# One projection's last 128 columns with exchanged operands, and a bias in a copy, in a two-layer decoder on one core

## The chip, the cores and the metric

One NeuronCore of a Trainium2 chip runs the whole program in one launch. The time is device time in microseconds. Below it is abbreviated us. The kernel before takes 1340.01 us (median of three runs, 1339.97 to 1340.18). The engines are named as in the profile: PE is the matrix engine, PEld its weight loads, DVE the vector engine, ACT the scalar engine, POOL GpSimd, and SP the engine that issues most DMAs; a "q" behind a name (SPq, ACTq) means the instruction stream that issues DMAs there.

## The reference

The input x has 2048 positions of 1024 features, in 32-bit floats. Layer 0 normalises x (RMSNorm), makes four projections of it, B, C, h and G, forms `(B * conv3(C * h)) * silu(G)` with a causal convolution of width 3, and adds its projection to x. From this stream, x1, a shared K and V come out of one projection. Layer 1 makes a query and a gate, runs stick-breaking attention with 8 heads of 64, and ends so:

```python
z = jnp.einsum("bhqd,bhkd->bhqk", qb, kf[:, :, :kl]) * scale
log_one_minus = jnp.where(mask, jax.nn.log_sigmoid(-z), 0.0)
rev = lax.cumsum(log_one_minus, axis=3, reverse=True)
weights = jnp.exp(jnp.where(mask, z + rev, -jnp.inf))
o = jnp.einsum("bhqk,bhkd->bhqd", weights, vf[:, :, :kl])
x = x + (o * jax.nn.silu(g)) @ w_out_b[j]
return _rmsnorm(x, norm_f)
```

The sum over the attention weights telescopes, so the kernel computes the output as "first v" (the value at a fixed position beside each block of queries) plus a product of the remaining weights with differences of neighbouring values.

## The kernel before

**Layout.** Everything lies transposed: features on the 128 partitions, positions along the free axis, in reversed order. The 2048 positions are four chunks (`c` = 0 to 3) of 512 columns (`CH`); 1024 features are eight blocks of 128 (`KD`, index `ob` or `k`). A full-precision product is built from split operands: each operand is kept as a high part and the rest (`split`, tiles of type float32r), and three matmuls (high with high, high with rest, rest with high) are added in PSUM; `mm3` does that over the contraction blocks. One matmul multiplies a stationary 128x128 block by a moving 128x512 block.

**Stages.** Layer 0's projections (tiles `fa_C`, `fa_B` and the like) use a scheme of seven products in place of eight, then comes its output projection (`fa_o`), the pair K/Q and V/G (`fa_kq`, `fa_vg`), then attention per chunk and head (`attend`, line 1056) and the last projection (`pob`): `out_kept` with `norm_kept` for chunks 0 to 2, and `out_last` (line 1328) for chunk 3.

**One head of attention.** PE makes `z`, ACT takes the sigmoid into `R`, POOL masks it, DVE scans it, PE transposes it into `wt`, ACT and DVE split it into `wth` and `wtl`, and PE multiplies by V into `av`. There is one PSUM bank for `av` (`NAV` is 1, line 32). `av` leaves it in two steps: an ACT copy of one half of its partitions into `ot`, then a DVE addition of the other half. The next head's first `av` matmul needs both done. After two heads `gate_kept` (line 1276) lets POOL add `v_first` to `ot` by blocks of 128 columns and multiply by the gate `sga`; for chunks 2 and 3 `split_og` then makes the operands `og` on ACT and DVE.

**The last chunk.** For each block `ob`, `out_last` runs 12 matmuls into `pob`, DVE adds them to `x`, ACT squares `x` into `sq_x` and scales `x` by the last norm's gain. The squares of the first five blocks are summed by POOL into `acc_x`; that sum and the last three squares go through matmuls with a column of ones into `pst_x`, four columns of it, one for each 128 positions. `rsqrt` turns these into reciprocal roots by 12 small DVE instructions in a row, each needing the one ahead (`v_x`, `t_x`, `yr_x`), `bcast` spreads them over the partitions by four transposes (`prb_x`, and once more as `prb_x23s` for ACT's copy `pbs`), and DVE (six blocks) and POOL (two) multiply `x`. Eight DMAs of 256 KB, half from SP and half from ACT's queue, write the output. Behind them comes a branch on a flag (line 1421) to a fallback that isn't taken with these inputs.

**Order.** The kernel is not issued in the order in which it is written. All operations are recorded (so nearly all have line 363 in the profile: tiles tell them apart), each belongs to a named part (`a30` is chunk 3's head 0, `g30` its first gate, `o3` is `out_last`, `fold` the splitting of the last weights), and `PLAN` gives each part two keys, between which its operations get their priorities. A list planner (`order`, line 290) goes through time with a price for each operation (`cost`, line 214), always taking the operation that can start first and, among those, the one with the lowest key. The result is one fixed instruction order for each engine, and every engine executes its own strictly in that order, waiting where an operand is late.

## Time and profile before

| what | before |
|---|---|
| median of three runs | 1340.01 us |
| the profiled execution, its own time | 1341.83 us |
| its span, first to last instruction | 1340.0 us |
| mean granted PE clock | 0.993 of full |
| PE busy | 1302.8 us, 97% |
| DVE busy | 1016.9 us, 76% |
| ACT busy | 599.7 us, 45% |
| POOL busy | 435.5 us, 33% |

The span runs from the first to the last instruction. Rows of groups give the line, engine, operation, output<-input, shapes and count, then busy time and the mean duration of one in ns, then the idle time of that engine just ahead and what ended it. The chain of waits follows the work back from the last instruction. A row of the stretches view begins with the stretch, its length, then busy us and count for PE, PEld, DVE, ACT and POOL, the PE clock granted, the DMA share and GB/s. In the order of time a row gives start, length, engine, and what ran.

### The profile page before, as it was taken

The numbers are of one execution on the slowest core, as the hardware profiler recorded it, in microseconds if no ns is written. First come the engines' busy times: TensorE is split into PE (matmuls) and PEld (weight loads), VectorE is DVE, ScalarE is ACT, GpSimd is POOL, SyncE is SP. The second block draws the span as 40 slices with busy tenths as digits, with TensorE's granted clock in tenths as the row PEclk, the third lists the DMA queues.
The fourth block names the chain that finished last, engine by engine and source line by source line (L and its number), as shares of the span: only waits on it lengthen the run. The fifth ranks groups of instructions, "written<-read, shape, count | busy, mean of one in ns | idle before, by whom it ended". The sixth has DMA issues, their size and how long they took to land.

```text
span 1340.0 us, 18973 instructions
## 1 busy us (share of the span) xinstructions
PE 1302.8 (97%) x6184; PEld 1078.0 (80%) x6184; DVE 1016.9 (76%) x1607; ACT 599.7 (45%) x1052; POOL 435.5 (33%) x553
## 2 busy tenths in 40 slices
PE   8999999999999999999999989999999999999996
PEld 6888888888888888888787777788778887788885
DVE  7899866689964655656869578877998886797855
ACT  7344534444432332323334334554555553566643
POOL 5252000001000000010032355334357675547982
PEclk9999999999999999999999999999999999999997
DMA  9439879878898799987998976887687567999734
GB/s 326 170 130 326 283 271 325 282 278 295 306 355 289 253 356 330 325 289 244 352 322 314 310 260 209 266 264 236 223 301 255 185 209 227 335 367 300 264 106 159
DMA packets 215292, 364.99 MB, mean 272 GB/s; under 512 B 16996, under 2 KB 101008, under 8 KB 215184
## 3 DMA queue, kind: packets, MB, share of 16 engines
q1 hardware_dynamic: 214464, 362.61, 79.4%
q8 instruction: 51, 0.84, 0.2%
q10 hardware_dynamic: 592, 1.05, 0.2%
q14 instruction: 57, 0.47, 0.1%
q0 software_dynamic: 128, 0.02, 0.0%
HBM read 217.35 MB, written 146.28 MB: 271 GB/s over the span
## 4 chain that ended last, share of the span: by engine, by line
PE 78%; DVE 12%; issue 4%; DMA 2%; POOL 2%; ACT 1%; SPq 0%; DVEq 0%; POOLq 0%; ACTq 0%
PE fa_C L363 11%; PE fa_B L363 10%; PE fa_o L363 6%; PE fd_C L363 6%; PE pob L363 5%; PE fd_B L363 5%; PE fa_kq L363 5%; PE fa_vg L363 4%; PE fe_C L363 3%; PE fd_vg L363 3%; PE fe_B L363 3%; PE fd_o L363 3%; PE fd_kq L363 3%; PE av L363 2%; PE wt L363 1%
## 5 line engine op out<-in xcount | busy, mean ns | idle before, releaser
L363 POOL COPY halo<-p 128x2 f32<-128x2 f32 x32 | 15.1, 472 | 435.2 <-DVE p L363 435.2
L363 POOL TENSOR_TENSOR acc_x<-acc_x,sq_x 128x512 f32<-128x512 f32 x53 | 75.4, 1427 | 132.0 <-ACT sq_x L363 127.4
L363 PE MATMUL pob<-og,wob 128*128 128x512 f32 x384 | 103.8, 403 | 0.6 <-DVE x L363 0.6
L363 PE MATMUL fa_C<-op_t,whl_s_C 128*128 128x512 f32 x336 | 83.3, 389 | 0.0
L363 PE MATMUL fa_B<-op_t,whl_s_B 128*128 128x512 f32 x336 | 82.4, 390 | 0.2 <-ACT f_B L363 0.2
L363 PEld LDWEIGHTS pob<-og,wob 128*128 128x128 f32 x384 | 67.6, 189 | 11.9 <-DVE x L363 1.1
L363 DVE TENSOR_TENSOR_SCAN R<-R,ones 128x192 f32<-128x192 f32 x128 | 74.2, 620 | 3.3 <-POOL R L363 3.2
L363 PEld LDWEIGHTS fa_B<-op_t,whl_s_B 128*128 128x128 f32 x336 | 62.9, 188 | 13.6 <-ACT f_B L363 0.6
L363 PEld LDWEIGHTS fa_C<-op_t,whl_s_C 128*128 128x128 f32 x336 | 63.0, 188 | 13.1
L363 DVE SCALAR_TENSOR_TENSOR cv<-p,cols_of,cv 128x512 f32<-128x512 f32 x64 | 50.2, 785 | 11.0 <-ACT cv L363 9.9
L363 ACT ACTIVATE sq_x<-x 128x512 f32<-128x512 f32 x56 | 35.1, 631 | 42.8 <-DVE x L363 32.1
L363 ACT ACTIVATE cv<-p,cols_of 128x512 f32<-128x512 f32 x32 | 23.2, 725 | 68.8 <-DVE p L363 68.8
L363 ACT CAST wth<-wt 128x512 fp32r<-128x512 f32 x64 | 36.4, 574 | 37.5 <-PE av L363 21.5
L363 DVE TENSOR_TENSOR wtl<-wt,wth 128x512 fp32r<-128x512 f32 x64 | 42.4, 667 | 12.4 <-ACT wth L363 11.6
L363 PE MATMUL wt<-ident,R 128*128 128x128 f32 x248 | 46.4, 274 | 1.0 <-DVE R L363 1.0
L363 PE MATMUL fa_C<-op_b,whl_a_C 128*128 128x512 f32 x168 | 43.1, 390 | 0.0
L363 PE MATMUL fa_B<-op_t,whl_a_B 128*128 128x512 f32 x168 | 43.0, 389 | 0.0
L363 PE MATMUL fe_B<-op_b,whl_a_B 128*128 128x512 f32 x168 | 42.9, 390 | 0.0
L363 POOL TENSOR_SCALAR_AFFINE_SELECT R<-R 128x256 f32<-128x256 f32 x64 | 34.9, 552 | 24.6 <-ACT R L363 24.3
L363 PE MATMUL fd_C<-op_t,whl_s_C 128*128 128x512 f32 x168 | 42.3, 390 | 0.1
L363 PE MATMUL fe_C<-op_b,whl_a_C 128*128 128x512 f32 x168 | 42.0, 389 | 0.0
L363 PE MATMUL fd_C<-op_b,whl_s_C 128*128 128x512 f32 x168 | 41.7, 390 | 0.0
(1019 smaller groups left out, 3807.5 us busy)
## 6 DMA issues: line engine op xcount, KB each, us to landing
sw_s_C<-whl_s_C SPq DMA_DIRECT2D x32, 512.0 KB, 4.3
sw_s_B<-whl_s_B SPq DMA_DIRECT2D x32, 512.0 KB, 4.4
q<-q_d SPq DMA_DIRECT2D x32, 512.0 KB, 5.8
sw_a_C<-whl_a_C SPq DMA_DIRECT2D x24, 512.0 KB, 3.5
sw_a_B<-whl_a_B SPq DMA_DIRECT2D x24, 512.0 KB, 3.6
whl_s_C<-sw_s_C SPq DMA_DIRECT2D x24, 512.0 KB, 5.4
whl_s_B<-sw_s_B SPq DMA_DIRECT2D x24, 512.0 KB, 5.4
whl_s_o<-sw_s_o SPq DMA_DIRECT2D x24, 512.0 KB, 5.6
```

The source lines that it names most:

```text
L363: getattr(o.engine.engine, o.name)(*map(real, o.args), **{k: real(v) for k, v in o.kw.items()})
```

## The change

Three things change.

First, in `attend` the ACT copy of half of `av` becomes four ACT instructions of 128 columns with `v_first` as a per-partition bias, and `gate_kept` loses POOL's addition.

Second, `out_last` computes only the first 384 columns of chunk 3 in the old way (96 matmuls with 384 moving columns, three columns of sums, three transposes for each spread). The last 128 positions are computed with the operands exchanged: `og` is stationary and the weights move, so that two PSUM banks (`last_0`, `last_1`) hold positions on partitions and 512 features each along the free axis. `x1` enters these banks by eight transposes (from `x1_end`, which DVE copies), 24 matmuls of 512 columns are added, ACT squares each bank with an accumulated sum along the free axis, 11 Newton instructions and a few around them follow, and a multiplication by a diagonal matrix `dg` (eight 32-bit matmuls of 128 columns, `back_0`, `back_1`) turns the result back and scales it. ACT and DVE apply the gain by blocks; two DMAs of 256 KB write it, and the other eight have 192 KB each. For this the last weights are stored as four tiles of 512 features per half (`ob_d`, `wob[half][k]`) in place of eight per-block tiles: `fold_gains` and `keep_ob` move as many bytes by as many DMAs.

Third, `PLAN` has new keys for most parts from the output projection of layer 0 on (`fold`, `w8`, `po02` and after), and two new parts, `n3` (the old part of the last norm) and `le` (the exchanged one). Keys of the parts ahead are as they were.

```diff
@@ -38,35 +38,35 @@
-    "s3": (-293.294, -20.5102), "fold": (800.991, 911.477), "w0": (62.4408, 469.025), "w1": (335.354, 455.789),
-    "w2": (368.335, 582.012), "w4": (62.6256, 146.045), "w8": (524.305, 703.505), "x2": (-30.2407, 35.8582),
...
-    "n0": (19.9786, 411.681), "o1": (1527.61, 1746.55), "n1": (665.062, 969.187), "o2": (1872.71, 1969.28),
-    "n2": (1218.33, 1322.06), "o3": (2272.7, 2273.2),
+    "s3": (-293.294, -20.5102), "fold": (766.008, 866.66), "w0": (62.4408, 469.025), "w1": (335.354, 455.789),
+    "w2": (368.335, 582.012), "w4": (62.6256, 146.045), "w8": (525.756, 631.744), "x2": (-30.2407, 35.8582),
...
+    "n0": (19.9786, 411.681), "o1": (1912.98, 1926.49), "n1": (1838.91, 2173.2), "o2": (2178.88, 2478.46),
+    "n2": (1887.69, 2977.04), "o3": (2473, 2652.93), "n3": (1034.66, 1050.15), "le": (2491.64, 2709.05),
@@ -227,7 +229,7 @@
         psum = any(isinstance(v, View) and v.base.pool.kind == "psum" for v in rest)
         o.turns = not psum and sum(isinstance(v, View) for v in rest) > 1 and (kind == DVE or kind == POOL and n > 8)
         if kind == PE:
-            if o.name == "transpose":
+            if o.name == "transpose" or o.kw.get("is_transpose"):
                 o.busy, o.late = 0.1085, 0.36
             else:
                 n = rest[1].extent()[1]
@@ -476,6 +478,9 @@
         v = sb.tile([P, 4], F32, name=f"v_{nm}", tag="sv")[:, 0:n]
         nc.vector.tensor_scalar(out=v, in0=ps[:, 0:n], scalar1=1.0 / D, scalar2=EPS, op0=ALU.mult, op1=ALU.add)
 
+        return newton(v, nm, y, n)
+
+    def newton(v, nm, y, n):
         if y is None:
             y = sb.tile([P, 4], F32, name=f"yr_{nm}", tag="sy")[:, 0:n]
         t = sb.tile([P, 4], F32, name=f"t_{nm}", tag="st")[:, 0:n]
@@ -938,16 +943,18 @@
                 use(cb, c + i, first, second)
 
 
+    ob_d = [[dram.tile([P, 2, CH], F32, name=f"sw_ob{i}_{k}") for k in range(4)] for i in range(2)]
+
     def fold_gains():
 
-        for ob in range(KD):
-            split_d["ob", ob] = [dram.tile([P, 2, 4, P], F32, name=f"sw_ob{ob}")]
-            raw = ld512(f"obr_{ob}").rearrange("p (k n) -> p k n", k=4)
-            hi, lo = (sb.tile([P, 4, P], F32R, name=f"fold{m}_ob{ob}", tag="og", bufs=KD) for m in range(2))
-            nc.sync.dma_start(out=raw, in_=w_out_b[0][:, ob * P:(ob + 1) * P].rearrange("(k p) n -> p k n", p=P))
-            split(hi, lo, raw)
-            for m, t in enumerate((hi, lo)):
-                nc.sync.dma_start(out=split_d["ob", ob][0][:, m], in_=t.bitcast(F32))
+        for half in range(2):
+            for k in range(4):
+                raw = ld512(f"obr_{half}_{k}")
+                hi, lo = (sb.tile([P, CH], F32R, name=f"fold{m}_ob{half}_{k}", tag="og", bufs=KD) for m in range(2))
+                nc.sync.dma_start(out=raw, in_=w_out_b[0][k * P:(k + 1) * P, half * CH:(half + 1) * CH])
+                split(hi, lo, raw)
+                for m, t in enumerate((hi, lo)):
+                    nc.sync.dma_start(out=ob_d[half][k][:, m], in_=t.bitcast(F32))
 
     kept = {}
 
@@ -1129,7 +1136,9 @@
                 j += n
         osl = slice(hi_ * 64, hi_ * 64 + 64)
         oth = slice(64 - hi_ * 64, 128 - hi_ * 64)
-        nc.scalar.copy(ot[osl, :], av[oth, :])
+        for b in range(4):
+            blk = slice(b * P, (b + 1) * P)
+            nc.scalar.activation(ot[osl, blk], av[oth, blk], AF.Identity, bias=v_first[osl, c, hb, b:b + 1])
         nc.vector.tensor_add(ot[osl, :], ot[osl, :], av[osl, :])
 
     def attention(c, h, ot):
@@ -1236,8 +1245,13 @@
 
     acc_b = {}
 
-    def load_ob(c, ob):
-        return load_w(None, ("ob", ob), f"ob{c}_{ob}", kt=4)
+    def mm3_ob(ps, ob, og, n=CH, wt=None):
+        i = 0
+        for k in range(4):
+            for w, m in ((0, 0), (0, 1), (1, 0)):
+                b = (wob[ob // 4][k] if wt is None else wt[k])[:, w, (ob % 4) * P:(ob % 4 + 1) * P]
+                nc.tensor.matmul(ps[:, 0:n], b, og[k][:, m, 0:n], start=i == 0, stop=i == 11)
+                i += 1
 
     def out_b(c):
         for k in range(4):
@@ -1265,18 +1283,17 @@
             nc.gpsimd.tensor_mul(t, t, pbs)
             nc.sync.dma_start(out=outT[k * P:(k + 1) * P, cols(c)], in_=t)
 
-    wob, x2_t = [], {}
+    wob, x2_t = [[], []], {}
 
     def keep_ob():
-        for ob in range(KD):
-            t = sb.tile([P, 2, Q, P], F32R, name=f"wob_{ob}", tag="act", bufs=NA)
-            nc.sync.dma_start(out=t.bitcast(F32), in_=split_d["ob", ob][0])
-            wob.append(t)
+        for half in range(2):
+            for k in range(4):
+                t = sb.tile([P, 2, CH], F32R, name=f"wob_{half}_{k}", tag="act", bufs=NA)
+                nc.sync.dma_start(out=t.bitcast(F32), in_=ob_d[half][k])
+                wob[half].append(t)
 
     def gate_kept(c, k, ot):
         sg = load_sg(c, k)
-        by_block = ot.rearrange("p (j k) -> p j k", j=4)
-        nc.gpsimd.tensor_add(by_block, by_block, v_first[:, c, k, :].unsqueeze(2).to_broadcast([P, 4, P]))
         nc.gpsimd.tensor_mul(ot, ot, sg)
         if c < 2:
             nc.sync.dma_start(out=og_d[c][k], in_=ot)
@@ -1327,46 +1344,93 @@
 
     def out_last(c):
 
+        n = CH - P
         x2 = x2_rows(c)
         acc = sb.tile([P, CH], F32, name=f"acc_x2{c}", tag="acc", bufs=2)
         ps2 = psum.tile([P, CH], F32, name=f"pst_x2{c}", tag="wt", bufs=NWT)
 
         def add_sums(t, first, last):
-            for j in range(4):
+            for j in range(3):
                 nc.tensor.matmul(ps2[:, j:j + 1], t[:, j * P:(j + 1) * P], ones[:, 0:1], start=first and j == 0,
-                                 stop=last and j == 3, skip_group_check=True)
+                                 stop=last and j == 2, skip_group_check=True)
 
         late = []
+        turned = sb.tile([P, 2, CH], F32, name="turned", tag="act", bufs=NA)
+        x1_end = sb.tile([P, KD, P], F32, name="x1_end", tag="q2", bufs=2)
         for ob in range(KD):
             x = x2[ob]
             nc.sync.dma_start(out=x, in_=x1_d[c][ob])
             tag, bufs = (("lin", NLIN), ("z", NZ))[ob % 2]
+            nc.vector.tensor_copy(x1_end[:, ob, :], x[:, n:CH])
             ps = psum.tile([P, CH], F32, name=f"pob_{c}_{ob}", tag=tag, bufs=bufs)
-            mm3(ps, wob[ob:ob + 1], og_t[c], kt=4)
+            mm3_ob(ps, ob, og_t[c], n)
             if late:
                 add_sums(late.pop(), ob == NACC + 1, False)
             if ob == NACC:
                 late.append(acc)
-            nc.vector.tensor_add(x, x, ps)
+            nc.vector.tensor_add(x[:, 0:n], x[:, 0:n], ps[:, 0:n])
             if ob < NACC:
-                square_into(acc, x, ob == 0, f"x2{c}{ob}", nc.gpsimd, ("wth", NWTS))
+                square_into(acc[:, 0:n], x[:, 0:n], ob == 0, f"x2{c}{ob}", nc.gpsimd, ("wth", NWTS), n)
             else:
                 sq = sb.tile([P, CH], F32, name=f"sq_x2{c}{ob}", tag=("wth", "wtl")[ob % 2], bufs=NWTS)
-                nc.scalar.activation(sq, x, AF.Square)
+                nc.scalar.activation(sq[:, 0:n], x[:, 0:n], AF.Square)
                 late.insert(0, sq)
-            nc.scalar.activation(x, x, AF.Copy, scale=gains["f"][:, ob:ob + 1])
-        while late:
-            add_sums(late.pop(), False, not late)
-        y = rsqrt(ps2, f"x2{c}")
-        pb = bcast(y, f"x2{c}")
+            nc.scalar.activation(x[:, 0:n], x[:, 0:n], AF.Copy, scale=gains["f"][:, ob:ob + 1])
+        ends = []
+        for half in range(2):
+            ps = psum.tile([P, CH], F32, name=f"last_{half}", tag=("lin", "z")[half], bufs=(NLIN, NZ)[half])
+            ends.append(ps)
+            for j in range(4):
+                nc.tensor.matmul(ps[:, j * P:(j + 1) * P], x1_end[:, 4 * half + j, :], ident, is_transpose=True, start=j == 0,
+                                 stop=False, skip_group_check=True)
+            i = 0
+            for k in range(4):
+                for w, m in ((0, 0), (0, 1), (1, 0)):
+                    nc.tensor.matmul(ps, og_t[c][k][:, m, n:CH], wob[half][k][:, w, :], start=False, stop=i == 11, skip_group_check=True)
+                    i += 1
+                if late:
+                    add_sums(late.pop(), False, not late)
+            if half == 0:
+                assert not late
+                y = rsqrt(ps2, f"x2{c}", n=3)
+        nc.part = "n3"
+        pb = bcast(y, f"x2{c}", n=3)
         pbs = t512(f"pbs_{c}")
-        nc.scalar.copy(pbs, bcast(y, f"x2{c}s"))
+        nc.scalar.copy(pbs[:, 0:n], bcast(y, f"x2{c}s", n=3)[:, 0:n])
         for k in range(KD):
-            if k in (2, 6):
-                nc.gpsimd.tensor_mul(x2[k], x2[k], pbs)
+            if k in (1, 3, 6):
+                nc.gpsimd.tensor_mul(x2[k][:, 0:n], x2[k][:, 0:n], pbs[:, 0:n])
             else:
-                nc.vector.tensor_mul(x2[k], x2[k], pb)
-            (nc.scalar if k % 2 else nc.sync).dma_start(out=outT[k * P:(k + 1) * P, cols(c)], in_=x2[k])
+                nc.vector.tensor_mul(x2[k][:, 0:n], x2[k][:, 0:n], pb[:, 0:n])
+            (nc.scalar if k % 2 else nc.sync).dma_start(out=outT[k * P:(k + 1) * P, S - CH * (c + 1):S - CH * c - P], in_=x2[k][:, 0:n])
+        nc.part = "le"
+        sums = const.tile([P, 2], F32, name="sums")
+        for half in range(2):
+            nc.vector.tensor_copy(turned[:, half, :], ends[half])
+            sq = sb.tile([P, CH], F32, name=f"sq_last_{half}", tag="kt", bufs=2)
+            nc.scalar.activation(sq, ends[half], AF.Square, accum_out=sums[:, half:half + 1])
+            if half == 0:
+                nc.vector.tensor_scalar(out=sums[:, 0:1], in0=sums[:, 0:1], scalar1=1.0 / D, scalar2=EPS, op0=ALU.mult, op1=ALU.add)
+        total = sb.tile([P, 4], F32, name="total", tag="sv")[:, 0:1]
+        nc.vector.scalar_tensor_tensor(out=total, in0=sums[:, 1:2], scalar=1.0 / D, in1=sums[:, 0:1], op0=ALU.mult, op1=ALU.add)
+        y = newton(total, "last", None, 1)
+        dg = sb.tile([P, P], F32, name="dg", tag="q2", bufs=2)
+        nc.vector.tensor_scalar(out=dg, in0=ident, scalar1=y, scalar2=None, op0=ALU.mult)
+        done = sb.tile([P, 2, CH], F32, name="done", tag="act", bufs=NA)
+        for half in range(2):
+            ps = psum.tile([P, CH], F32, name=f"back_{half}", tag=("lin", "z")[half], bufs=(NLIN, NZ)[half])
+            for j in range(4):
+                nc.tensor.matmul(ps[:, j * P:(j + 1) * P], turned[:, half, j * P:(j + 1) * P], dg, start=True, stop=True)
+            for j in range(4):
+                ob = 4 * half + j
+                blk = slice(j * P, (j + 1) * P)
+                if j % 2:
+                    nc.vector.tensor_scalar(out=done[:, half, blk], in0=ps[:, blk], scalar1=gains["f"][:, ob:ob + 1], scalar2=None, op0=ALU.mult)
+                else:
+                    nc.scalar.activation(done[:, half, blk], ps[:, blk], AF.Copy, scale=gains["f"][:, ob:ob + 1])
+            (nc.scalar if half else nc.sync).dma_start(
+                out=outT[4 * half * P:4 * (half + 1) * P, S - CH * c - P:S - CH * c].rearrange("(k p) n -> p k n", p=P),
+                in_=done[:, half, :].rearrange("p (k n) -> p k n", k=4))
```

20 lines of the change are left out of this document (13 added, 7 removed), and 42 rows, old and new, of the table PLAN.

## The prediction

> **What bounds the kernel now.** I read the totals and the chain of waits first, then stretches, then the end in order of time.
>
> ```profile
> span 1340.0 us, 18973 instructions
> PE 1302.8 (97%) x6184; PEld 1078.0 (80%) x6184; DVE 1016.9 (76%) x1607; ACT 599.7 (45%) x1052; POOL 435.5 (33%) x553
> ...
> PE 78%; DVE 12%; issue 4%; DMA 2%; POOL 2%; ACT 1%; SPq 0%; DVEq 0%; POOLq 0%; ACTq 0%
> ```
>
> PE is busy 97% of the span and carries 78% of the chain, so only two things can shorten this kernel: PE's idle time, and the end, where PE has nothing left. Stretches (PE, PEld, DVE, ACT, POOL, clock, DMA) say where the idle time is:
>
> ```profile
> 0.00:600.00 600.00, 592.21 (x2619) 488.01 (x2620) 441.28 (x694) 240.19 (x411) 85.03 (x111) 1.00 0.84 288
> 600.00:1000.00 400.00, 389.34 (x1751) 317.29 (x1750) 319.78 (x484) 175.09 (x306) 134.72 (x124) 1.00 0.82 276
> 1000.00:1290.00 290.00, 284.48 (x1623) 241.28 (x1622) 233.46 (x375) 167.03 (x308) 192.10 (x300) 1.00 0.75 252
> 1290.00:1321.50 31.50, 31.50 (x164) 26.58 (x163) 16.68 (x36) 14.99 (x26) 21.19 (x17) 1.00 0.58 201
> 1321.50:1340.00 18.50, 5.26 (x34) 4.80 (x33) 5.72 (x19) 2.37 (x4) 2.50 (x2) 0.56 0.33 119
> ```
>
> Idle PE time: 600 - 592.21 = 7.8 us up to 600, 10.66 from 600 to 1000, 5.52 from 1000 to 1290, none from there to 1321.5, 13.24 in the end. The middle 10.66 + 5.52 = **16.2 us** are what another order can win; the first 7.8 lie ahead of every changed key. The end, by the chain of waits (start, length):
>
> ```profile
> 1312.66 8.21 PE pob L363 x36
> 1320.87 3.97 PE pst_x L363 x32
> ...
> 1324.86 0.17 DVE v_x L363
> ...
> 1327.03 0.17 DVE yr_x L363
> ...
> 1327.34 1.10 PE prb_x L363 x4
> ...
> 1328.53 0.70 DVE x L363
> ...
> 1331.20 1.27 POOL x L363
> ```
>
> The last projection ends at 1320.87. Then 32 records of column sums (3.97), 12 DVE instructions from 1324.86 to 1327.20 (0.197 each), the spread, the multiplications up to 1331.20 + 1.27 = 1332.47, and DMAs, by a stretch and by the DMA queue's own waits:
>
> ```profile
> 1330.00:1336.00 6.00, 0.00 (x0) 0.00 (x0) 2.20 (x4) 0.00 (x0) 2.47 (x2) 0.50 0.98 351
> ...
> SPq L1421 <- SPq L1421: 3.8, 1, 3.8
> ```
>
> DMA engines are full for these 6 us; the branch closes the program in 3.8 us, so the last data has landed by 1336.2, **3.7 us** behind the last multiplication.
>
> **The change part by part: the end.** Prices for PE come from the spacing of starts, where 128x256 matmuls follow each other, and from one transpose in the chain:
>
> ```profile
> 1298.74 0.28 PE L363 MATMUL av<-wtl,vv 128*128 128x256 f32 x1
> 1298.86 0.28 PE L363 MATMUL av<-wth,vv 128*128 128x256 f32 x1
> ...
> 1296.17 0.11 PE wt L363
> ```
>
> A 256-column matmul takes 0.12, a 512-column one 8.21 / 36 = 0.228, so one of 384 lies halfway: 0.174. PE then needs, against today's 1320.87: 96 x (0.174 - 0.228) = -5.2; 24 exchanged matmuls +5.5; eight transposes of `x1_end` +0.9; 24 records of sums (three columns, not four) at 3.97 / 32 = 0.124, +3.0; six spread transposes +0.7. The last projection then ends at **1325.7**. The 384-column norm (2.4 of DVE, five multiplications of about 0.5 on DVE and three on POOL) starts when sums are done, with two thirds of the exchanged matmuls still to come, some 4 us of cover; without it, 2.5 us of multiplications would queue on DVE ahead of the second norm. Of the eight DMAs that follow, four are issued by ACT and can stand ahead of its last square, each behind the multiplication it waits for; I take it that the planner puts them where these are done. Eight copies of 128 columns into `x1_end` (about 2.3 us together) fall into the stretch where DVE is busy 16.68 of 31.5, and the two copies out of the banks lie beside ACT's squares.
>
> Behind 1325.7: the square 0.62 (row below), the joining instruction and 11 Newton instructions 12 x 0.197 = 2.4, `dg` 0.3 (a DVE instruction on 128 columns, between the tiny 0.17 and the 0.70 for 512), hand-overs 0.3, the `back` matmuls, one gain block 0.3. No 32-bit matmul with 128 moving columns stands in this trace. The nearest: `pst_x` shows 32 records for its 16 matmuls, so two each; and a record with 128 columns at the clock granted here is `prb_x`, 1.10 / 4 = 0.275. The clock:
>
> ```profile
> 1318.00:1321.40 3.40, 3.40 (x20) 2.93 (x19) 1.97 (x4) 3.00 (x6) 1.29 (x1) 1.00 0.95 345
> 1321.50:1323.70 2.20, 2.20 (x22) 2.20 (x21) 0.09 (x1) 1.78 (x3) 0.00 (x0) 0.99 0.00 0
> 1323.80:1324.80 1.00, 1.00 (x5) 0.93 (x5) 0.00 (x0) 0.00 (x0) 0.00 (x0) 0.50 0.00 0
> ```
>
> It halves 2.9 us behind the last projection and stays there; `back` starts 3.6 us behind it, so I take half clock: 8 x 2 x 0.275 = **4.4**. Bounds: full clock, 8 x 2 x 0.11 = 1.8; four records each at half clock, 8.8. I stay with two records, since that is what the rows of the same operand type show. The last gain block ends at 1325.7 + 0.6 + 2.4 + 0.3 + 0.3 + 4.4 + 0.3 = 1334.0, against 1332.47 today: +1.5. In exchange the DMA backlog is gone, since 1.5 MB leave earlier and the two last DMAs carry 0.25 MB each:
>
> ```profile
> DMA to landing us min/median/max: 2.5/3.4/5.4
> ```
>
> Landing can fall from 3.7 to 2.5; I take the middle, -0.6. **The end: about +0.8 us**, from -1.8 with `back` at full clock to +5.2 with four records. The hidden norm is paid for by sums that PE now does ahead of its end, by transposes, and by a second norm with the same row of small DVE steps.
>
> A rule that speaks against the change: the Trainium skill, "FP8 and Floating Point Precision", section "TensorE Precision Notes", says that true 32-bit matmuls take four passes through the array. Taken as four records, that is the upper bound of 8.8, and the kernel would come out at 1340.4 in place of the forecast; the trace's two records per matmul speak for less, but with one moving column they can't show how long two passes inside a record take.
>
> **The bias in ACT's copy**, by groups of ACT and POOL and, last, one row in order of time:
>
> ```profile
> L363 ACT ACTIVATE sq_x<-x 128x512 f32<-128x512 f32 x56 | 35.1, 631 | 42.8 <-DVE x L363 32.1 <-DMA whl_a_o<-sw_a_o 6.1 <-issue 1.6
> L363 ACT ACTIVATE R<-z 128x384 f32<-128x384 f32 x64 | 29.8, 492 | 7.7 <-PE z L363 7.5
> L363 ACT ACTIVATE x<-x,cols_of 128x512 f32<-128x512 f32 x32 | 22.8, 721 | 0.7
> L363 ACT COPY ot<-av 64x512 f32<-64x512 f32 x32 | 18.6, 582 | 18.8 <-PE av L363 18.4
> ...
> L363 POOL TENSOR_TENSOR ot<-ot,v_first 128x512 f32<-128x512 f32 x16 | 18.1, 1130 | 4.4 <-DVE ot L363 4.0 <-PE fd_vg L363 0.4
> ...
> 1312.29 1.14 ACT L363 ACTIVATE sq_x<-x 128x512 f32<-128x512 f32 x2
> ```
>
> From 384 to 512 columns is 582 - 492 = 90 ns, so 128 columns take 582 - 270 = 312; a column operand adds 721 - 631 = 90: 0.40 for one. Two in a row overlap by 2 x 0.63 - 1.14 = 0.12, so four take 4 x 0.40 - 3 x 0.12 = 1.25 where the copy took 0.58: **+0.67 us in each of 32 heads** (0.1 if an instruction cost only its columns, 1.0 without overlap). ACT has room, 167 of 290 us. But behind this copy wait DVE's addition, everything behind that on DVE, and then PE's next `av` matmul, on the one bank. In 11 of the 32 heads that matmul starts within 0.65 us of the addition's end. The first and the last of them:
>
> ```profile
> 1182.98 0.67 DVE L363 TENSOR_TENSOR ot<-ot,av 64x512 f32<-64x512 f32 x1
> ...
> 1183.70 0.39 PE L363 MATMUL av<-wth,vv 128*128 128x256 f32 x1 [0.24 <-DVE ot L363]
> ...
> 1297.61 0.68 DVE L363 TENSOR_TENSOR ot<-ot,av 64x512 f32<-64x512 f32 x1
> ...
> 1298.63 0.28 PE L363 MATMUL av<-wth,vv 128*128 128x256 f32 x1
> ```
>
> Their slacks run from 0.05 to 0.61, and in five the addition was late for another reason; 0.67 less both, added up over the 11, is 2.35 us in today's order. The order is new and knows of four instructions, so I take half: **+1.2** (0 to 2.35). POOL's 16 x 1.13 us go away, off PE's path in today's order: nothing gained directly, though `og` is ready sooner after the last head.
>
> **The weights' layout** moves as many bytes in as many issues on SP (8 loads, 16 stores, 8 reloads), past the same queue; at nothing, since PE's waits here are not for these tiles.
>
> **The order.** Of the 16.2 us, two places have DVE itself full (rows of ten us: PE, PEld, DVE):
>
> ```profile
> 780.00:790.00 10.00, 6.55 (x28) 4.80 (x27) 10.00 (x12) 3.03 (x6) 3.98 (x3) 1.00 0.76 280
> ...
> 1160.00:1170.00 10.00, 8.73 (x55) 7.01 (x53) 9.65 (x19) 5.83 (x12) 5.76 (x15) 1.00 1.04 396
> 1170.00:1180.00 10.00, 9.01 (x64) 8.07 (x65) 8.60 (x16) 5.56 (x12) 5.38 (x16) 1.00 1.00 345
> 1180.00:1190.00 10.00, 9.40 (x76) 8.39 (x75) 9.91 (x18) 7.44 (x16) 4.17 (x13) 1.00 1.04 392
> ```
>
> That is 3.45 + 1.27 + 0.99 + 0.60 = 6.3 us; the other **9.9 us** are short waits for an operand that arrives late while its engine had room, which other keys can remove. Nothing in the profile tells how many; a new order can also make new ones. I take 6 of the 9.9, a judgement between 0 and 9.9.
>
> **Sum**, against the profiled span of 1340.0, which the median of the runs (1340.01) matches, though that profiled execution itself took 1341.83 with what lies around the span: 1340.0 + 0.8 + 1.2 - 6.0 = **1336.0 us**.
>
> **The rivals.** (1) *The gains cancel*: the order wins nothing and the end and the copy stand alone, 1340 + 0.8 + 0 to 1.2 = 1341; or the order wins its 6 and `back` takes four records, 1336 + 4.4 = 1340.4. For it: every gain that I count comes from keys whose effect no row shows. Against it: the parts between 600 and 1290, where the waits are, all have new keys. (2) *The bank held by ACT decides*: from the point where the slack behind an addition falls below 0.67, each such head stops PE, and no wait is won back; 1340 + 0.8 + 2.4 = 1343.2, more if more heads are tight than 11. For it: the planner's price for an ACT instruction adds 0.09 for a column scale, none for a column bias. Against: PE's waits for `av` are few today. (3) *The clock holds*: if it halves 3.6 us or more behind the last projection, not 2.9, `back` runs at full clock, 1336 - 2.6 = 1333.4. For it: the time from dense work to the drop is known from one drop alone. Against: the row above. The Trainium skill, "TensorE: Matmul & The Clock Gate", section "Part 1: The HAM clock gate", has the clock judged in free-running windows of about 3.4 us; by that the drop can come at any time inside one, and this rival would be a matter of phase; the trace's 2.9 us fits. (4) *Nearly all 9.9 us go*, copy absorbed: about 1330.
>
> **How the numbers follow.** A measurement tells some 0.2%, 2.7 us, from no change. Forecast 0.38 (own range 1333 to 1338), (1) 0.24, (2) 0.20, (3) 0.10, (4) 0.08. Faster: 0.38 + 0.10 + 0.08 = 0.56; same 0.24; slower 0.20. The range goes from 1340 - 1.8 - 9.9, about 1328.5, to rival (2), 1343.
>
> **What would show it.** Right: PE's last dense matmul about 15 us ahead of the end, or later by the chain; `back` records near 0.27 at half clock; four ACT instructions near 0.4 each on `ot`; PE's idle time from 600 to 1320 near 10 us. Wrong: idle time there still 16 or more, `av` matmuls waiting for DVE's `ot` in many heads, DVE's multiplications running into the second norm, or an end (from the last dense matmul) well off 15.1 us (1340.8 - 1325.7).

## The result and the profile after

The changed kernel takes **1352.74 us** (median of 4 runs, 1351.48 to 1354.51), the kernel before took 1340.10 beside it: a ratio of 1.0086 (1.0072 to 1.0099), so **slower by about 12 us**. 1336.0 was forecast, and the time lies outside the range of 1328.5 to 1343.

The profiled execution of the changed kernel took 1353.53 us by its own time, with a span of 1351.7. From its page, the totals (busy time, share, instructions):

```profile
PE 1312.6 (97%) x6222; PEld 1081.7 (80%) x6222; DVE 1019.9 (75%) x1634; ACT 622.9 (46%) x1156; POOL 420.4 (31%) x538
```

PE is busy 9.8 us longer than before (1312.6 - 1302.8). The stretches of the same execution, in the columns of the prediction's (PE, PEld, DVE, ACT, POOL, clock, DMA):

```profile
0.00:600.00 600.00, 592.37 (x2617) 487.95 (x2618) 444.24 (x697) 240.56 (x412) 86.98 (x111) 1.00 0.82 287
600.00:1000.00 400.00, 392.68 (x1778) 321.15 (x1777) 322.10 (x492) 181.13 (x320) 137.54 (x127) 1.00 0.83 282
1000.00:1290.00 290.00, 279.90 (x1571) 231.16 (x1570) 216.55 (x356) 175.50 (x373) 167.68 (x279) 1.00 0.73 245
```

Up to 600 nothing has moved. From 600 to 1290 PE is idle for 7.3 + 10.1 = 17.4 us, where 16.2 stood and 10 were forecast. The gain of 6 us has not come; 600 to 1000 has improved by 3.3 us, and 1000 to 1290, the stretch of most heads, has lost 4.6. What PE waits for is shown by two lines of the waits (who waits, for whom, us in total, times, longest), first of PE's weight loads, then of its matmuls:

```profile
PEld av L365 <- ACT ot L365: 13.4, 26, 0.9
...
PE av L365 <- ACT ot L365: 5.8, 14, 0.7
```

No such line stands in the trace of before. The `av` matmuls wait for ACT's reads into `ot`, the four instructions that carry the bias. The last head in order of time shows how:

```profile
1298.85 0.36 ACT L365 ACTIVATE ot<-av,v_first 64x128 f32<-64x128 f32 x1
...
1299.26 0.33 PE L365 MATMUL av<-wth,vv 128*128 128x128 f32 x1 [0.38 <-ACT ot L365]
...
1299.62 0.36 ACT L365 ACTIVATE ot<-av,v_first 64x128 f32<-64x128 f32 x1 [0.42 <-PE av L365]
...
1300.03 0.33 PE L365 MATMUL av<-wtl,vv 128*128 128x128 f32 x1 [0.16 <-ACT ot L365]
...
1300.40 0.36 ACT L365 ACTIVATE ot<-av,v_first 64x128 f32<-64x128 f32 x1 [0.42 <-PE av L365]
1300.79 0.69 DVE L365 TENSOR_TENSOR ot<-ot,av 64x512 f32<-64x512 f32 x1 [0.20 <-ACT ot L365]
```

PE and ACT take turns: a matmul into the bank, a read of a finished block of it, the next matmul, the next read. A 512-column copy could only stand behind all matmuls of the head. Reads of 128 columns can be planned as soon as their own block is finished, and the planner does so; but the later matmuls write other columns of the *same* PSUM bank, and the waits are kept for the bank and not for columns. The order of the instructions says the same without any time: 67 of the `av` matmuls carry a wait for ACT, where 47 did; in the last head the read of one block of 128 columns is waited for by a matmul that writes another.

Of this mechanism there is a rule in the Trainium skill: "PSUM — Partial Sum Buffer", section "PSUM bank collisions raise a hardware error", has PSUM guarded by bank and quadrant of partitions, not by address. The trace agrees with it: the waits above are between different columns of one bank.

The end, by the chain of waits (start, length, and the number of instructions where there are several):

```profile
1307.83 9.11 PE pob L365 x51
...
1339.84 1.67 PE back L365 x6
...
1341.52 0.38 ACT done L365
...
1341.94 2.09 PE back L365 x8
...
1344.06 0.38 ACT done L365
...
1344.48 0.81 PE back L365 x2
...
1346.10 0.35 DVE done L365
```

A 384-column matmul takes 9.11 / 51 = 0.179 us (0.174 estimated). The 16 `back` records are stopped twice by ACT's `done` instruction, which reads the bank that the next `back` matmul writes: the same turn as in `av`. And in order of time the last dense matmul, the five multiplications of the 384-column norm on DVE, the three on POOL, the copy out of the second `last` bank, and the instruction that joins the two sums of squares:

```profile
1333.51 2.41 DVE L365 TENSOR_TENSOR x<-x,prb_x 128x384 f32<-128x384 f32 x5 [0.70 <-PE prb_x L365]
...
1333.56 1.41 PE L365 MATMUL last<-wob,og 128*128 128x512 f32 x5
...
1334.40 2.92 POOL L365 TENSOR_TENSOR x<-x,pbs 128x384 f32<-128x384 f32 x3 [14.03 <-ACT pbs L365]
...
1335.84 0.68 DVE L365 COPY turned<-last 128x512 f32<-128x512 f32 x1
...
1336.44 0.89 DVE L365 SCALAR_TENSOR_TENSOR total<-sums 128x1 f32<-128x1 f32 x1
```

Dense work ends at 1333.56 + 1.41 = **1334.97**, and the span 16.7 us later; 1325.7 without the bias and the order, and 15.1, were worked out. `total`, on one column, takes 0.89 and ends at 1337.33, just as POOL's third multiplication does (1337.32).

### The profile page after: what moved, and what is told of

Read it like the earlier page. It is cut to its first block, busy times and chain, and to the rows that moved or that the text cites. A ratio compares the mean times of both kernels' runs of the same rounds, so it can differ in the third digit from the quotient of the medians.

```text
span 1351.7 us, 19169 instructions
## 1 busy us (share of the span) xinstructions
PE 1312.6 (97%) x6222; PEld 1081.7 (80%) x6222; DVE 1019.9 (75%) x1634; ACT 622.9 (46%) x1156; POOL 420.4 (31%) x538
## 5 line engine op out<-in xcount | busy, mean ns | idle before, releaser
L365 POOL TENSOR_TENSOR acc_x<-acc_x,sq_x 128x512 f32<-128x512 f32 (+1 forms) x53 | 74.1, 1404 | 125.3 <-ACT sq_x L365 122.4
L365 PE MATMUL pob<-og,wob 128*128 128x512 f32 (+1 forms) x384 | 100.0, 391 | 1.9 <-DVE og L365 1.9
L365 PEld LDWEIGHTS pob<-og,wob 128*128 128x128 f32 x384 | 66.4, 189 | 10.1 <-DVE og L365 2.6
L365 ACT ACTIVATE ot<-av,v_first 64x128 f32<-64x128 f32 x128 | 40.3, 358 | 30.8 <-PE av L365 29.1
L365 ACT ACTIVATE sq_x<-x 128x512 f32<-128x512 f32 (+1 forms) x56 | 34.4, 617 | 39.3 <-DVE x L365 32.5
```

The source lines that it names most:

```text
L365: getattr(o.engine.engine, o.name)(*map(real, o.args), **{k: real(v) for k, v in o.kw.items()})
```

## The experiments

Three theories were set against each other. (1) PE waits for ACT's reads of the one `av` bank in the middle of a head. (2) The new order and the longer end cost the time, whatever the bias does. (3) ACT's additional work itself costs it. Each run is compared with the kernel before on the same chip, whose median was 1342.22 beside the first four runs below, 1341.37 beside the one read, the load behind the copy and the clock held on purpose, and 1341.58 beside the others. Where a text says that an order stays, the change is made while the planned order is being issued, since an edit of the source would have it planned anew; the diff then shows what the change amounts to in the source.

**The changed kernel with the reads held back.** The orders of PE, DVE, POOL and SP stay as in the changed kernel; on ACT each bias read moves behind the last matmul of its bank.

```diff
-    ops = nc.order(PLAN)
+    ops = hold(nc.order(PLAN), lambda o: o.engine.name == ACT and isinstance(o.kw.get("bias"), View))
```

> The changed kernel in its own order on PE, DVE, POOL and SP; only ACT's bias reads of av that stood ahead of the bank's last matmul are moved behind it. Theory 1 (PE waits for ACT's reads of the one av bank in the middle of a head; 13.4 us of weight-load idle, some 8.5 us of it lost): about 1344. Theory 2 (the new order and the longer end cost it): 1352 to 1353, as the changed kernel. Theory 3 (ACT's extra work itself, 23 us more busy, holds the chain): 1352 or more, since the reads now come later still.

Measured: 1345.09 us (1343.58 to 1347.58), a ratio of 1.0024 (1.0012 to 1.0035). By the two ratios, 0.62% or 8.3 us of the changed kernel's time are gone, with the same instructions on every engine. That shows theory (1) for the changed kernel. In its waits no line of `av` for ACT's `ot` is left, while the weight loads of `av` wait for `wth`, ACT's other product in a head, as long as before (2.5 us, 2.4 in the changed kernel), so it is not ACT's queue that the early reads had held up; the last head's addition comes eight microseconds earlier than the 1300.79 above. The second row is PE's time from its first `av` matmul to the end of dense work:

```profile
1292.97 0.69 DVE L368 TENSOR_TENSOR ot<-ot,av 64x512 f32<-64x512 f32 x1 [0.52 <-ACT ot L368]
...
921.41:1325.46 404.05, 393.59 (x2165) 328.49 (x2163) 319.91 (x520) 237.07 (x498) 234.04 (x341) 1.00 0.73 244
```

**The changed kernel without the bias.** The four reads become the one copy again, where the last of them stood once held back; POOL adds the first v again. Everything else, the order too, is as in the changed kernel.

```diff
-        for b in range(4):
-            blk = slice(b * P, (b + 1) * P)
-            nc.scalar.activation(ot[osl, blk], av[oth, blk], AF.Identity, bias=v_first[osl, c, hb, b:b + 1])
+        nc.scalar.copy(ot[osl, :], av[oth, :])
...
+        nc.gpsimd.tensor_add(by_block, by_block, v_first[:, c, k, :].unsqueeze(2).to_broadcast([P, 4, P]))
         nc.gpsimd.tensor_mul(ot, ot, sg)
```

> The changed kernel in its own order, with one ACT copy per head (behind the last matmul) and POOL's 16 additions back in place of the bias reads. Theory 1: about 1343, like the kernel with the reads held or 1 us less. Theory 2: 1351 to 1353. Theory 3: about 1343, but then the kernel with held reads stays at 1352.

Measured: 1343.57 us (1342.70 to 1345.97), ratio 1.0013 (1.0003 to 1.0023). So of the changed kernel's loss of 0.86%, the bias makes up 0.73%, about 10 us, and theory (2) is left with 0.13%. Held back, the bias would cost 0.11%, 1.5 us, which the two intervals hardly tell from nothing. Stretches of this kernel, its last dense matmuls, PE's time from the first `av` matmul to the end of dense work, and `av` alone on PE (sum over the stretches up to 1321.5):

```profile
600.00:1000.00 400.00, 393.89 (x1793) 322.03 (x1792) 326.80 (x494) 181.59 (x317) 139.74 (x131) 1.00 0.83 282
1000.00:1290.00 290.00, 281.10 (x1607) 236.65 (x1607) 228.70 (x366) 161.72 (x298) 191.08 (x295) 1.00 0.74 250
...
1323.72 1.40 PE L381 MATMUL last<-wob,og 128*128 128x512 f32 x5
...
921.72:1325.12 403.40, 391.19 (x2165) 329.17 (x2163) 324.37 (x520) 220.09 (x402) 251.76 (x357) 1.00 0.72 245
...
sum 1321.50, PE 51.34; mean PE 12.83
```

The last two of these for the changed kernel, and a stretch of it from an earlier stage:

```profile
780.00:790.00 10.00, 9.47 (x35) 7.63 (x36) 6.84 (x11) 5.93 (x10) 2.79 (x3) 0.83 0.68 243
924.22:1334.97 410.75, 397.01 (x2165) 328.78 (x2163) 316.01 (x520) 241.15 (x498) 232.67 (x341) 1.00 0.71 240
...
sum 1321.50, PE 55.39; mean PE 13.85
```

Dense work ends at 1325.12 here, 9.85 us ahead of the changed kernel's 1334.97. Where are these 9.85? The first `av` matmul already starts 2.5 us later there, at 924.22 for 921.72, and no bias read stands ahead of it. In that profiled execution the granted clock is 0.83 from 780 to 790, so half for 2 x 0.17 x 10 = 3.4 us, which can cost 1.7; this kernel shows 1.00 there with the same instructions. These 2.5 us go with the execution, not with the bias. The bias has the rest, 410.75 - 403.40 = **7.35 us**, so 7 to 10 us between the traces and the medians (6.7 and 8.3 of it are gone when the reads are held back, by 404.05 and by the ratios). Of the 7.35, PE's idle time makes 1.5 (13.74 for 12.21), though the waits for ACT's `ot` alone are 5.8: other waits have become shorter. *Busy* time makes 5.8 (397.01 for 391.19), and 4.05 = 55.39 - 51.34 of that lie in the same 304 `av` matmuls: a record lasts some 0.28 us, and started 0.12 apart several lie over each other, while after a stop one stands alone. So the loss must not be read from idle time only. Idle time from 600 to 1290 is 6.1 + 8.9 = 15.0 us here, 1.2 less than before; from 1290 to the end of dense work it is 1.5, where none stood.

**The kernel before with the bias, reads late and early.** Its order stays exactly; POOL's additions go, and the copy becomes four reads, at the copy's own place, or each as soon as the last matmul of its block has been issued.

```diff
-        nc.scalar.copy(ot[osl, :], av[oth, :])
+        for b in range(4):
+            blk = slice(b * P, (b + 1) * P)
+            nc.scalar.activation(ot[osl, blk], av[oth, blk], AF.Identity, bias=v_first[osl, c, hb, b:b + 1])
...
-        nc.gpsimd.tensor_add(by_block, by_block, v_first[:, c, k, :].unsqueeze(2).to_broadcast([P, 4, P]))
```

> The kernel before in its own order, with four bias reads in the copy's place (so all behind the last matmul) and POOL's additions out. Theory 1: 1340 to 1342.5, the price of late av banks alone, up to 2.4 us. Theory 2: 1340 to 1342. Theory 3: 1346 or more.

> As the one with four bias reads in the order of before, but each read is given to ACT as soon as the last matmul of its own 128 columns has been issued, so that most stand ahead of later matmuls of the same bank. Theory 1: 8 to 20 us slower than with late reads, 1350 to 1360, and PE's weight loads wait for ACT's reads of av. Theory 2: as with late reads, 1340 to 1342. Theory 3: as with late reads, 1346.

Measured: late 1349.32 us, ratio 1.0050 (1.0032 to 1.0068); early **1406.59 us**, ratio 1.0471 (1.0444 to 1.0498). Early, 110 `av` matmuls carry a wait for ACT, and the waits (PE's weight loads, PE) are

```profile
PEld av L374 <- ACT ot L380: 46.6, 68, 1.1
...
PE av L374 <- ACT ot L380: 31.4, 63, 0.9
...
1000.00:1290.00 290.00, 262.30 (x1339) 211.50 (x1340) 194.97 (x304) 156.19 (x325) 130.96 (x232) 0.95 0.68 222
```

The same four instructions, only earlier, cost 57 us more, far above the 8 to 20 that were expected, and the waits grow with the loss: theory (1) holds in the old order too. Not all of the 57 us is PE's wait for the bank. An early read also stops ACT's own queue until the matmul ahead of it is done (80.4 us idle ahead of these reads, 17.0 with late ones). And between its stops PE's clock falls: the last row has 0.95 granted, half for 2 x 0.05 x 290 = 29 us, which can cost 14.5; before it had 1.00. No run parts these three. The late reads, though, were to cost no more than 2.35 us and cost 7, while 47 waits of `av` for ACT are as many as before. The reads themselves last about as long as estimated:

```profile
L380 ACT ACTIVATE ot<-av,v_first 64x128 f32<-64x128 f32 x128 | 35.9, 356 | 18.0 <-PE av L374 17.0 <-POOL R L374 0.7
...
1309.12 1.11 ACT L380 ACTIVATE ot<-av,v_first 64x128 f32<-64x128 f32 x4 [0.92 <-PE av L374]
```

Four in a row take 1.11 (1.25 estimated) where the copy took 0.58. The size per head was about right, and the place where it costs was not. Two more runs are to find it.

**One read of 512 columns with a bias; and the old copy with ACT's additional work behind it.** Both in the order of before. The one read leaves out three of the four biases: it adds the first block's to all columns, and POOL's additions are gone. In the second kernel they stay.

```diff
-        nc.scalar.copy(ot[osl, :], av[oth, :])
+        nc.scalar.activation(ot[osl, :], av[oth, :], AF.Identity, bias=v_first[osl, c, hb, 0:1])
```

```diff
         nc.scalar.copy(ot[osl, :], av[oth, :])
+        for _ in range(3):
+            nc.scalar.activation(idle[osl, :], ones[osl, :], AF.Identity, bias=left_bias[osl, :])
```

> The kernel before in its own order, POOL's additions out, the copy replaced by one ACT instruction of 512 columns with a column bias (the first block's value for all four blocks, so three blocks get another block's bias). Four late reads cost 7 us against before. If that is the number of instructions (1.5 us of ACT per head against 0.6): 1341 to 1343, as before. If it is the missing additions on POOL or the bias operand: 1347 to 1350.

> The kernel before with the copy and POOL's additions as they were, and three ACT instructions of 128 columns on constant data behind each copy, so that ACT's stream is as late as with four bias reads while the av bank comes free at its old time. They write to a tile that nothing reads. If the four reads cost through ACT's stream (the next head's casts and sigmoids come late): 1347 to 1351. If they cost through the bank that is held: 1341 to 1343.

Measured: one read 1342.27 us, ratio 1.0007 (0.9998 to 1.0017); load behind the copy 1357.36 us, ratio 1.0119 (1.0104 to 1.0135). ACT's groups in the one and in the other:

```profile
L380 ACT ACTIVATE ot<-av,v_first 64x512 f32<-64x512 f32 x32 | 21.9, 683 | 18.0 <-PE av L374 17.6
```

```profile
L365 ACT ACTIVATE idle<-ones,left_bias 64x128 f32<-64x128 f32 x96 | 38.4, 400 | 2.4
```

In the second kernel the bank comes free with the copy, as before, and PE still loses 16 us; the only thing that is late is what stands behind on ACT. These three instructions are more than the lateness of four reads, for which they were meant: 1.2 us per head (38.4 / 32) for 0.53, and the loss is larger alike, 16 for 7; 5 to 10 had been expected. In the first, 0.10 us more per head costs nothing that can be told, so neither the bias nor the missing additions on POOL cost the 7. So in a fixed order the price is paid mainly in ACT's queue: ACT results that PE needs come later, head by head. (The bank has a small part: weight loads of `av` wait 2.2 us for DVE's `ot` with late reads, 0.6 before.) By the start of the addition, the late reads are 0.8 us behind the kernel before in the first head of all and 9.7 in the last:

```profile
1300.56 0.69 DVE L363 TENSOR_TENSOR ot<-ot,av 64x512 f32<-64x512 f32 x1 [2.27 <-ACT ot L363]
```

```profile
1310.27 0.69 DVE L374 TENSOR_TENSOR ot<-ot,av 64x512 f32<-64x512 f32 x1 [2.63 <-ACT ot L380]
...
1170.00:1180.00 10.00, 8.55 (x39) 6.96 (x38) 8.28 (x15) 5.29 (x14) 5.28 (x17) 0.67 1.02 364
```

The last row belongs to the late reads: the granted clock is 0.67 there, half for 2 x 0.33 x 10 = 6.6 us, which can cost 3.3; the kernel before has 1.00, with PE busy 9.01. The load behind the copy and the one read have such a drop in the same ten microseconds (0.74 and 0.71), and the one read comes out like before in spite of it. So the share of the clock in the 7 and the 16 stays open.

Theory (3) holds in the old order, then, and not in the new one, which was planned with the four instructions in it and pays at most some 1.5 us for them when they are held back.

**The exchange alone.** The changed program without the bias, planned with the keys of before and those that the new parts need (the keys themselves are left out here).

```diff
...
-            nc.scalar.activation(ot[osl, blk], av[oth, blk], AF.Identity, bias=v_first[osl, c, hb, b:b + 1])
+        nc.scalar.copy(ot[osl, :], av[oth, :])
...
+        nc.gpsimd.tensor_add(by_block, by_block, v_first[:, c, k, :].unsqueeze(2).to_broadcast([P, 4, P]))
         nc.gpsimd.tensor_mul(ot, ot, sg)
```

> The kernel before with the exchanged last columns and the weights' new layout, its own keys (the two new parts take theirs from the change), no bias in ACT: the copy and POOL's additions stay. If the exchange itself is about neutral, as the prediction's sum for the end says (+0.8), and the new keys win nothing: 1341 to 1344 where before takes 1340 to 1342. If the new keys cost something beside the bias: at or below before, 1339 to 1341. If the exchange costs more than its sum: 1345 or more. The planner makes a new order from the old keys, so one to three us of this can be the order's.

Measured: 1354.58 us, ratio 1.0098 (1.0085 to 1.0112). The expectation was 1341 to 1344. This is not simply the price of the exchange, since the same exchange takes 1343.57 in the order of the new keys. The planner makes quite another order from old keys and a changed program. Up to 1000 PE is idle no more than before (10.45 us from 600, for 10.66); what it loses stands behind, 8.19 us from 1000 to 1290 for 5.52, and 3.23 from there to the end of dense work at 1334.70 for none, with a granted clock of 0.92:

```profile
600.00:1000.00 400.00, 389.55 (x1759) 317.59 (x1759) 319.69 (x486) 176.52 (x309) 134.49 (x125) 1.00 0.81 277
1000.00:1290.00 290.00, 281.81 (x1601) 238.12 (x1600) 227.10 (x366) 163.06 (x302) 190.17 (x298) 1.00 0.74 251
1290.00:1334.70 44.70, 41.47 (x232) 37.68 (x230) 24.33 (x70) 17.76 (x34) 21.79 (x19) 0.92 0.39 142
```

What the new keys give by themselves, and what the exchange costs in a given order, can't be read from it and stays open.

**A shorter end.** POOL takes two of the multiplications, not three; the copy out of each `last` bank goes to ACT behind the square; and one DVE instruction per bank replaces the four `done` blocks. It was tried on the kernel of the last experiment and on the one without the bias. Beside them, the changed kernel with both the bias reads and the `done` reads held back behind their banks' last matmuls.

```diff
-            if k in (1, 3, 6):
+            if k in (1, 3):
...
-            nc.vector.tensor_copy(turned[:, half, :], ends[half])
             nc.scalar.activation(sq, ends[half], AF.Square, accum_out=sums[:, half:half + 1])
+            nc.scalar.copy(turned[:, half, :], ends[half])
...
-            for j in range(4):
...
+            nc.vector.tensor_mul(done[:, half, :].rearrange("p (j k) -> p j k", j=4), ps.rearrange("p (j k) -> p j k", j=4), gf)
```

> As the one with the exchange alone, and its end shortened: one DVE multiplication of 512 columns per back bank in place of four instructions on ACT and DVE in turns, the copies out of the two banks on ACT behind its squares, and two multiplications on POOL in place of three. If readers of one bank wait for each other and POOL holds DVE's first step of the second norm (0.89 where its like take 0.16), 1.5 to 2.5 us less than with the exchange alone; if these waits are covered, no difference.

> The changed kernel's keys, the bias taken out again, and the same shortened end: 1.5 to 2.5 us less than 1343.6, so 1341 to 1342, which is no more than the time of before; no difference to 1343.6 if the waits in the end are covered.

> The changed kernel with both the bias reads and the eight gain blocks held behind the last matmul of their bank; looked at for the end alone. From the first back matmul to the last DMA issue the changed kernel takes 1346.48 - 1339.84 = 6.6 us. If matmuls of a back bank wait for reads of its other columns, the wait goes (0.46 us twice) but four reads in a row follow the last matmul: 5.6 to 6.2. If that wait is the clock's or the weight load's, 7 or more.

Measured: 1351.30 us, ratio 1.0073 (1.0059 to 1.0086), so 3.3 us less than without the shorter end; 1340.99 us, ratio 0.9997 (0.9988 to 1.0006), about 2 us less than 1.0013; and 1343.13 us in a single execution for the last, which has no interval. From the last, then the second:

```profile
1330.90 3.78 PE L368 MATMUL back<-dg,turned 128*128 128x128 f32 x16 [4.86 <-DVE dg L368]
...
1336.29 0.39 ACTq L368 DMA_DIRECT2D out_dram<-done  x1
```

```profile
1325.13 0.15 DVE L381 SCALAR_TENSOR_TENSOR total<-sums 128x1 f32<-128x1 f32 x1
...
1327.87 2.58 PE L381 MATMUL back<-dg,turned 128*128 128x128 f32 x16 [3.62 <-DVE dg L381]
...
1327.80:1330.50 2.70, 2.58 (x16) 2.32 (x16) 0.70 (x2) 0.00 (x0) 0.00 (x0) 0.75 0.08 23
```

Held back, the 16 `back` records take 3.78 without a stop, where they took from 1339.84 to 1345.29; but the `done` blocks then follow behind: 5.4 us from the start of `back` to the last DMA's issue, against 6.6 in the changed kernel (1346.48 - 1339.84). In the second kernel `total` is back at 0.15, with POOL done at 1325.19 (two multiplications, 1.97 us from 1323.22), and `back` takes 2.58: by the 0.75 of the last row the granted clock halved in the middle of it, some 1.35 us into the row (1.35 + 1.35 / 2 = 0.75 x 2.7), at about 1329.15.

**The clock held on purpose.** The kernel without the bias and with the shorter end, and ten matmuls into a spare bank, whose result nobody reads, behind the last exchanged matmul.

```diff
+        warm = psum.tile([P, CH], F32, name="warm", tag="wt", bufs=NWT)
+        for i in range(10):
+            nc.tensor.matmul(warm, og_t[c][0][:, 0, n:CH], wob[0][0][:, 0, :], start=i == 0, stop=i == 9, skip_group_check=True)
...
```

> The kernel with the new keys, no bias and the shortened end, and ten matmuls of 512 columns into a spare bank between the last projection and the back matmuls; nothing reads their result. If PE's clock is what the back matmuls pay for, they take about 2.1 us at full clock, every time, where half clock would make it 4.2: up to 2 us less than without, most in the runs that were slow, so 1338 to 1340 with a narrower spread. If the clock falls anyway, or the back matmuls are not bound by it: 1341 as without, or 0.5 more.

Measured: 1339.40 us (1336.86 to 1340.31), ratio **0.9983** (0.9974 to 0.9992): this version is faster than the kernel before by about 2 us, and by the two ratios than the changed kernel by 1.03%, 14 us. Beside the same kernel without the ten matmuls (0.9997, 0.9988 to 1.0006) the intervals overlap a little. In order of time, and a stretch:

```profile
1324.96 2.44 PE L381 MATMUL warm<-wob,og 128*128 128x512 f32 x10
...
1328.65 2.05 PE L381 MATMUL back<-dg,turned 128*128 128x128 f32 x16 [1.25 <-DVE dg L381]
...
1327.00:1331.00 4.00, 2.45 (x18) 1.86 (x16) 2.30 (x10) 0.59 (x1) 0.00 (x0) 1.00 0.50 177
```

## Why the prediction was wrong

The forecast of a span of 1336.0 missed 1351.7 by 15.7 us. The profiled executions divide them so: 7.35 - 1.2 = 6.15 in the bias, 6.0 - 0.6 = 5.4 in the order, 16.7 - 15.1 = 1.6 in the end, and 2.5 that stand ahead of the first `av` matmul and go with the one execution.

- **The bias in ACT's copy, +1.2, is the step that failed.** Its cost is 7.35 us from the first `av` matmul to the end of dense work, with and without it, and about 10 by the medians. The 0.67 us per head were about right (1.11 - 0.58 = 0.53). What failed is the sentence that only the bank at the *end* of a head, and the 11 heads that follow it closely, could turn this into time. The four instructions were costed as a row in the place of the copy, but the change also lets them move, in between the matmuls of the bank; the step didn't ask where the planner may put them. Held at the copy's place, they cost some 1.5 us in the new order, inside the 0 to 2.35; in the old order 7, mainly through ACT's stream behind them. "ACT has room, 167 of 290 us" was the wrong argument for both: a share of busy time says nothing of what comes late behind a longer instruction in a fixed order.
- **The order, -6.0,** gave 0.6 by the end of dense work without the bias (1325.12 against 1325.7), and by the idle time 1.2 up to 1290, with 1.5 lost behind. That is nothing beyond what executions differ by: the one of before has a granted clock of 0.83 from 725 to 735, worth up to 1.7 us, where the kernel without the bias has 1.00. The forecast had said that no row tells how many of the 9.9 us go. The planner's keys are not a term that can be read from a profile of before, and rival (1), that the order wins nothing, was nearer on this point: 1341 was its time, and the kernel without the bias took 1.0013 times the time of before, with the longer end.
- **The end, 15.1 us behind dense work,** took 16.7. The terms: from the last dense matmul to the end of `total` 2.4 where the square, the joining instruction and a hand-over make 0.9; Newton and `dg` 2.5, as estimated; `back` 5.4, not 4.4, with two stops for ACT's reads; then 1.2 of gain blocks in turns, not 0.3; and 5.2, not 6.9, from there to the end. The first of these was put down as copies that lie beside ACT's squares, with the 384-column norm covered. It isn't covered. Its 12 small steps run from 1329.08 to 1332.81, 3.7 us for 2.4, because the copy `turned` of the first bank and a step that waits for ACT's square stand between them in DVE's order; its five multiplications then end at 1333.51 + 2.41 = 1335.92, 0.95 behind dense work. The second `turned` stands behind these, and `total` behind it for POOL. This is one of the forecast's own signs of being wrong. Its own figures said as much: 2.4 and five times 0.5 are 4.9 us, against 4 of cover. (Its sum for the end, 1.5 - 0.6, is 0.9 where it has 0.8; nothing hangs on that.)

Not covered as assumed were also the eight copies into `x1_end`, put at 2.3 us together: two of them in a row take 2.27 us from 1303.80, ahead of the `og` that the first 384-column matmul waits 0.71 us for.

Right were: the price of a 384-column matmul, 0.179 for 0.174 (the end of dense work, 1325.12 for 1325.7, agrees only if the order won nothing, so it can't count beside the bullet on the order); two records for a 32-bit matmul with 128 columns, 16 in all, so that the upper bound of four fell; and the clock at half speed in `back` of the changed kernel:

```profile
1337.50:1339.80 2.30, 0.00 (x0) 0.00 (x0) 1.90 (x12) 0.00 (x0) 0.00 (x0) 0.68 0.74 267
1339.80:1345.30 5.50, 4.52 (x16) 3.64 (x16) 0.70 (x2) 1.10 (x3) 0.00 (x0) 0.50 0.09 27
```

If it halved once in the first of these rows, that was 0.8 us into it (0.8 + 1.5 / 2 = 0.68 x 2.3), 3.4 us behind dense work, where 2.9 were read before. Rival (3), the clock that holds, is real but did not decide here. Rival (2), the bank held by ACT, had the right bank and the right two engines, and the wrong place: it started from the slack behind the addition, and came to 1343.2. Whether the planner's missing price for a column bias, which it named, had a part in where the reads were put, no run tested.

Left open: what the new keys alone give, the exchange in the exact order of before, which was not tried, and how much of each loss is the clock that falls where PE stops.

## What to carry to other kernels

When one instruction that reads a whole PSUM bank is cut into several, ask first where the pieces may now go: a read of a finished block ahead of a later matmul of the same bank stops PE, though the columns differ. Keep the pieces behind the bank's last matmul, which gave 8.3 us here; banks of their own for the blocks would be another way, not tried here. And price an added instruction by what stands behind it on its engine, not by the engine's free share.

## What the runs showed of the hardware

- A DVE instruction on one column took 0.89 us where such a one takes 0.15, and ended as POOL's multiplications did (1337.33 and 1337.32 above). With one multiplication less on POOL it took 0.15. The Trainium skill, "SBUF — State Buffer", section "SBUF: two separate sides", has DVE and GpSimd share a pair of ports as an exclusive lock: of a GpSimd instruction that reads SBUF and a DVE instruction with two SBUF inputs, the one that starts second waits for the other's whole length. `total` has two such inputs, and the trace agrees.
- A square with a sum takes a second instruction on ACT, 0.19 us, ahead of any DVE instruction that needs the sum; it did not stand in the estimate.

```profile
1335.00 0.60 ACT L365 ACTIVATE sq_last<-last 128x512 f32<-128x512 f32 x1 [0.68 <-PE last L365]
1335.50 0.19 ACT L365 ACTIVATION_READ_ACCUMULATOR sq_last<-last 128x1 f32 x1
```

- The time from dense work to the clock's drop is not fixed: 2.9 us before, about 3.4 in the changed kernel, and in the kernel with the shorter end and no bias, whose dense work ends at 1322.38 + 1.87 = 1324.25, about 4.9 (1329.15 above). The Trainium skill, "TensorE: Matmul & The Clock Gate", section "Part 1: The HAM clock gate", has the clock judged in free-running windows, which leaves the moment to their phase; the three times fit that, and no run changed the phase alone. `back` took 2.05 us at full clock and 3.78 at half. Ten matmuls, 2.44 us together, in the gap were enough to hold the clock at 1.00.

```profile
1322.38 1.87 PE L381 MATMUL last<-wob,og 128*128 128x512 f32 x7
```

- The clock also falls in the middle of the kernel, and not in every execution: 0.83 in 780 to 790 of the changed kernel, so half for 3.4 us, and 1.00 there without the bias, in the same order of instructions, with PE busy 9.47 and 9.67 of the ten.
